# One subtraction of a weight split is queued later on VectorE, at three stage ends of a two-layer decoder trunk

## The chip, the cores and the metric

The kernel runs on one NeuronCore of a Trainium2 chip. The metric is the device time of one execution in microseconds. A core has five engines that work through their own instruction queues: TensorE (PE, with its weight loads listed as PEld), VectorE (DVE), ScalarE (ACT), GpSimd (POOL) and SyncE (SP); the last two mostly issue DMA transfers here. Engines wait for each other by semaphores. An instruction that waits holds up everything behind it on its engine.

## The reference

The program is a decoder trunk of two layers, width 1024, on 512 tokens, in float32. One layer is

```
hn = rms_norm(h, g_ffn1) * (1 + sc1) + sh1
h  = h + 0.5 * (1 + gt1) * (silu(hn @ W_gate) * (hn @ W_up)) @ W_out      # ffn1
hn = rms_norm(h, g_mix) * (1 + sc2) + sh2
h  = h + (1 + gt2) * concat(attention, rwkv7, short_conv)(hn @ W_mix) @ W_mixout
hn = rms_norm(h, g_ffn2) * (1 + sc3) + sh3
h  = h + 0.5 * (1 + gt3) * (silu(hn @ W_gate') * (hn @ W_up')) @ W_out'   # ffn2
```

`sh`, `sc` and `gt` come from a small product with the condition vector `c`. The feed-forward width is 2816.

## The kernel before

**Data.** Activations lie with channels on the 128 partitions and the 512 tokens along the free dimension: the residual `h` is eight channel blocks of 128x512. Float32 products are made of three TensorE products each: every operand is parted into a high half (rounded to the format that TensorE takes) and a low half (what is left), and `mm3` (L125) issues high x high (L129), high activation low half x high weight (L130) and high activation x low weight (L131). In the profile the halves are `hnH`, `hnL` for the normed rows, `actH`, `actL` for the rows inside a feed-forward stage, and `wH`, `wL` for weights. A set of weights is one 128x1024 tile: eight blocks of 128x128, one per channel block. `split` (L138) parts a set with a cast on ScalarE (L141, writes `wH`) and a subtraction on VectorE (L143, writes `wL`).

**Stages.** Six stages run in turn: ffn1, mix, ffn2 of layer 0 and the same of layer 1. Each ends by computing the normed rows of the next. This text is about the end of a feed-forward stage, which three of the four feed-forward stages have in this form (the last one has no successor and returns earlier).

**The end of a feed-forward stage** (L691 to L731). The last two output blocks, 6 and 7, are computed in halves of the tokens (`HALVES`: the first 256, then the second 256), so that the first half can be normed while the second is still being multiplied. For each half, `residual` (L343) adds block 6 to `h`, then block 7. When a half is complete:

- `stats` sums the squares by a product with ones (`ps_ss`, L273), then takes a root on ScalarE (L275) and a reciprocal on VectorE (L276).
- `spread` brings the reciprocal to all partitions (`ps_rstd`, L283, TensorE).
- `apply` makes the eight channel blocks of normed rows. Per block: VectorE scales `h` (`hn_t`, L290), ScalarE adds the shift and rounds (`hnH`, L291), VectorE takes the low half (`hnL`, L292).

The sum of squares over blocks 0 to 6 is gathered in `ss` on VectorE (L250, after a square on ScalarE, L254); block 7 is added in `stats` itself.

The next stage begins with three sets of weights at once. The end of the stage before loads them into `raws` and `next_weights` splits them: the first set early, the second and the third beside the first half's `stats`. A fourth set is split by the code of the next stage (`load_w`, L299).

**What sets the order.** The code is recorded by a layer that then places each engine's instructions by its own estimate of when they are ready, in the order of the code where nothing else speaks. `queue_behind(name)` (L135) asks for a place behind the instruction last noted under that name: `act` and `dve` are notes of the norm's steps on ScalarE and VectorE, `norm_act` and `norm_dve` of the last L291 and L292. So a moved line in the code can move other instructions too, and the order that was built is what counts.

```
def next_weights(n):
    for w in raws[len(nxt) : n]:
        nxt.append(tuple(wp.tile([P, KD, P], F32R, name=x, tag=x, bufs=4) for x in ("wH", "wL")))
        split(*nxt[-1], w, ("act", "dve"))
```

Of the kernel before, what the change touches and what calls it, by code (L numbers as in the profile page):

```python
# [8 lines left out]
F32 = mybir.dt.float32  # L9
F32R = mybir.dt.float32r  # L10
# [7 lines left out]
P = 128  # L18
# [3 lines left out]
KD = D // P  # L22
# [48 lines left out]
def trunk_kernel(ctx, tc, ins, out, layers=L, phases=("ffn1", "mix", "ffn2")):  # L71
    nc = tc.nc
# [4 lines left out]
    wp = ctx.enter_context(tc.tile_pool(name="wp", bufs=3))  # L77
# [6 lines left out]
    act, mm = nc.scalar.activation, nc.tensor.matmul  # L84
# [10 lines left out]
    def psmm(tags=("mm",)):  # L95
        turn[0] += 1
        return psum([P, T], "ps_mm", tags[turn[0] % len(tags)])
# [27 lines left out]
    def mm3(acc, w, k, x, sl, start, stop):  # L125

        wH, wL, xH, xL = w[0][:, k], w[1][:, k], weave(x[0][:, sl]), weave(x[1][:, sl])
        acc = paired(acc)
        mm(acc, wH, xH, start=start, stop=False)  # L129
        mm(acc, wH, xL, start=False, stop=False)  # L130
        latest["large"] = mm(acc, wL, xH, start=False, stop=stop)  # L131
# [3 lines left out]
    def queue_behind(name):  # L135
        return tc.issue_after(latest[name].ins) if name in latest else nullcontext()

    def split(hi, lo, src, behind=None):  # L138
        a, d = behind or (None, None)
        with queue_behind(a):  # L140
            latest["cast"] = nc.scalar.copy(hi, src)  # L141
        with queue_behind(d):
            return nc.vector.tensor_sub(lo, src, hi.bitcast(F32))  # L143

    ALL = slice(0, T)
    HALVES = (slice(0, T // 2), slice(T // 2, T))
# [78 lines left out]
    def ada_steps(pool, crep, n, behind=None):  # L225

        cols = []
        for _ in todo[:n]:
            ada_turn[0] += 1
            cols.append(ada_load(pool.tile([P, D], F32, name="wada", tag=("first", "third", "sum1")[ada_turn[0] % 3], bufs=1)))  # L230
        ada_sums(cols, crep, behind)


    def ada_until(pool, crep, l, i):
        while todo and todo[0] <= (l, i, KD - 1):
            ada_steps(pool, crep, 1)
# [104 lines left out]
    def residual(pt, i, gate, ss, sl=ALL):  # L341
        hs = inorder(h[i][:, sl])
        done = stt(hs, Woven(pt).view, gate[:, i : i + 1], hs, ALU.mult, ALU.add)  # L343
        add_ss(ss, i, sl)
        return done

    def last_residual(pt, i, gate, ss, sl):

        residual(pt, i, gate, None, sl)
        return None if ss is None else square(i, sl)  # L350

    def ffn(l, w_in, w_pair, w_out, hn, im, ss, need, then, first, ready, coming):
# [6 lines left out]
        with tc.tile_pool(name="act", bufs=1) as ap_:  # L359
# [263 lines left out]
            late = ((5, 0), (7, 1), (10, "P1"), (12, "P2"), (13, "T3"), (14, "T4"))  # L623
# [73 lines left out]
            raws, nxt = [], []  # L697
# [4 lines left out]
            def next_weights(n):  # L702
                for w in raws[len(nxt) : n]:
                    nxt.append(tuple(wp.tile([P, KD, P], F32R, name=x, tag=x, bufs=4) for x in ("wH", "wL")))
                    split(*nxt[-1], w, ("act", "dve"))

            ada_until(ap_, crep, *need)
            stats, spread, apply = then()
            sqs = []
            for sl in HALVES:  # L710
                for i in (6, 7):
                    pt = psmm(BANKS[1:3])[:, : T // 2]
                    for j in range(j0, j1):
                        mm3(pt, last[i, j0 + (j - j0) // n * n], (j - j0) % n, xs[j], sl, j == j0, j == j1 - 1)
                        if sl is HALVES[1]:
                            if (i, j) == (6, j0 + 5):
                                stats(HALVES[0], sqs)
                                next_weights(3)
                            elif (i, j) == (7, j0):
                                spread(HALVES[0])  # L720
                                apply(HALVES[0])
                    if i == 6:
                        residual(pt, i, cg, ss, sl)
                        if sl is HALVES[0]:
                            next_weights(1)
                    else:
                        sqs = [last_residual(pt, i, cg, ss, sl)]
# [891 lines left out]
    for n, (l, p) in enumerate(seq):  # L1619
        im = what[p][1]  # L1620

        coming = ()
        if n + 1 < len(seq):
            l1, p1 = seq[n + 1]
            coming = [ins["wmi"][l1, t] if p1 == "mix" else ins[p1.replace("ffn", "w") + "i"][l1, t // 2, t % 2] for t in range(3)]
        nss = new_ss() if n + 1 < len(seq) else None
        nxt = []

        def then():
            if nss is None:  # L1630
                return [lambda *_: None] * 3
            nhn, scale, *steps = normed(n + 1, nss)
            nxt.append(nhn)
            scale()
            return steps

        if p == "mix":
            with tc.tile_pool(name="mix", bufs=1) as mp:
                ready = mix(l, hn, nss, mp, then, ready) or ()
        else:  # L1640
            w, need = ("w1", (l, 6)) if p == "ffn1" else ("w2", (l + 1, 1))
            ready = ffn(l, ins[w + "i"], ins[w + "p"], ins[w + "o"], hn, im, nss, need, then, first, ready, coming)
        first = None
        hn = nxt[0] if nxt else None
# [86 lines left out]
```

## Time and profile before

| what | value |
|---|---|
| median of 3 timed runs | 1795.22 us (1794.1 to 1796.64) |
| the profiled execution's own time | 1792.58 us |
| its span, first to last instruction | 1790.8 us |
| TensorE busy | 1766.0 us, 99% |
| VectorE busy | 1384.6 us, 77% |
| ScalarE busy | 856.5 us, 48% |
| first feed-forward end (ffn1, layer 0, to mix) | about 340 to 370 us |
| second end (ffn2, layer 0, to ffn1 of layer 1) | about 895 to 924 us |
| third end (ffn1, layer 1, to mix) | about 1224 to 1254 us |

Rows of the timeline give start and duration in us, the engine, the source line, the operation with what it writes and reads, and in brackets how long the engine stood idle before it and what ended that. A row with x2 or x3 is a run of equal instructions. The starts of neighbouring TensorE products lie closer than their durations, since products overlap; the step from start to start is what one costs. Rows of the windows view give, for a stretch of time, the busy time of each engine, the granted TensorE clock (PEclk, 1.00 is full speed) and the DMA share.

### The profile page before, as it was taken

The page shows a single profiled execution, that of the slowest core. Times are in us where ns is not written, and L with a number is a line of the kernel's source. Part 1 is how long each engine was busy: PE and PEld are TensorE (multiplying, and loading weights), DVE is VectorE, ACT ScalarE, POOL GpSimd, SP SyncE. Part 2 cuts the span into 40 slices and gives each one's busy share as a digit, 9 for nine tenths or more (in the row PEclk, how much of TensorE's full clock was granted, in tenths as well). Part 3 has the DMA queues.
Part 4 walks back from the last instruction along what each step waited for, and adds up shares of the span by engine and source line. Part 5 has one row for each costly group of instructions (what it writes and reads, how often), then busy time and mean ns, then how long its engine had stood idle before and what let it go on. Part 6 is the DMA issues. An engine that isn't in the chain of part 4 may idle for free.

```text
span 1790.8 us, 34026 instructions
## 1 busy us (share of the span) xinstructions
PE 1766.0 (99%) x13952; PEld 1613.3 (90%) x13952; DVE 1384.6 (77%) x2224; ACT 856.5 (48%) x1324; POOL 148.3 (8%) x233
## 2 busy tenths in 40 slices
PE   9999999999999999999999999999999999999998
PEld 7898999987778999899899989999877798999998
DVE  7877678867768877677888776887686788864897
ACT  7452354364444554255355514543654345533563
POOL 0101001101000001100100020010000000010000
PEclk9999999999999999999999999999999999999999
DMA  9667867523133666877737687773321427684764
GB/s 378 219 185 265 227 191 214 188 76 91 42 120 100 172 192 219 265 199 202 246 96 203 175 294 199 200 228 116 112 67 39 142 80 204 183 243 133 202 172 112
DMA packets 95436, 313.08 MB, mean 175 GB/s; under 512 B 10864, under 2 KB 13168, under 8 KB 94256
## 3 DMA queue, kind: packets, MB, share of 16 engines
q1 hardware_dynamic: 65088, 203.68, 33.8%
q0 software_dynamic: 30192, 107.23, 24.2%
q8 instruction: 109, 1.79, 0.4%
q14 instruction: 47, 0.39, 0.1%
HBM read 306.93 MB, written 3.93 MB: 174 GB/s over the span
## 4 chain that ended last, share of the span: by engine, by line
PE 85%; DVE 9%; ACT 3%; issue 2%; DMA 2%; SPq 0%; DVEq 0%; ACTq 0%
PE ps_mm L129 14%; PE ps_mm L130 14%; PE ps_mm L131 14%; PE ps_d L434 7%; PE ps_d L436 7%; PE ps_d L435 7%; PE ps_f L436 3%; PE ps_f L435 3%; PE ps_f L434 3%; DVE wL L143 2%; PE ps_mm L1546 2%; PE ps_g L436 2%; PE ps_g L435 2%; PE ps_g L434 2%; ACT wH L141 1%
## 5 line engine op out<-in xcount | busy, mean ns | idle before, releaser
L141 ACT CAST wH<-wraw 128x1024 fp32r<-128x1024 f32 (+2 forms) x276 | 254.3, 928 | 441.1 <-PE ps_mm L130 188.7
L143 DVE TENSOR_TENSOR wL<-wraw,wH 128x1024 fp32r<-128x1024 f32 (+2 forms) x276 | 295.4, 1074 | 112.6 <-ACT wH L141 111.8
L129 PE MATMUL ps_mm<-actH,wH 128*128 128x512 f32 (+1 forms) x700 | 253.6, 362 | 1.0 <-DVE h L343 1.0
L130 PE MATMUL ps_mm<-actL,wH 128*128 128x512 f32 (+1 forms) x700 | 252.8, 361 | 0.0
L131 PE MATMUL ps_mm<-actH,wL 128*128 128x512 f32 (+1 forms) x700 | 252.8, 361 | 0.0
L129 PE MATMUL ps_mm<-hnH,wH 128*128 128x512 f32 (+1 forms) x712 | 248.5, 354 | 3.3 <-ACT hnH L291 3.0
L130 PE MATMUL ps_mm<-hnL,wH 128*128 128x512 f32 (+1 forms) x712 | 246.4, 348 | 0.3
L131 PE MATMUL ps_mm<-hnH,wL 128*128 128x512 f32 (+1 forms) x712 | 245.5, 346 | 0.6 <-DVE wL L143 0.6
L434 PE MATMUL ps_d<-comH,wH 128*128 128x256 f32 x864 | 238.5, 276 | 0.0
L435 PE MATMUL ps_d<-comL,wH 128*128 128x256 f32 x864 | 237.6, 275 | 0.0
L436 PE MATMUL ps_d<-comH,wL 128*128 128x256 f32 x864 | 237.6, 275 | 0.0
L143 DVE TENSOR_TENSOR wL<-sum,wH 128x1024 fp32r<-128x1024 f32 x110 | 134.6, 1225 | 80.3 <-ACT wH L141 80.2
L199 DVE SCALAR_TENSOR_TENSOR wada<-wada,crep 128x1024 f32<-128x1024 f32 x128 | 153.3, 1221 | 31.6 <-DMA wada<-in_wadaT 30.9
L141 ACT CAST wH<-sum 128x1024 fp32r<-128x1024 f32 x110 | 115.1, 1047 | 120.2 <-PE ps_f L435 39.3
L434 PEld LDWEIGHTS ps_d<-comH,wH 128*128 128x128 f32 x864 | 165.8, 192 | 1.7 <-ACT s L460 1.6
L436 PEld LDWEIGHTS ps_d<-comH,wL 128*128 128x128 f32 x864 | 165.9, 192 | 0.0
L435 PEld LDWEIGHTS ps_d<-comL,wH 128*128 128x128 f32 x864 | 165.9, 192 | 0.0
L129 PEld LDWEIGHTS ps_mm<-hnH,wH 128*128 128x128 f32 x712 | 134.2, 191 | 23.7 <-issue 7.6
L131 PEld LDWEIGHTS ps_mm<-hnH,wL 128*128 128x128 f32 x712 | 136.0, 191 | 13.9 <-DVE wL L143 1.0
L130 PEld LDWEIGHTS ps_mm<-hnL,wH 128*128 128x128 f32 x712 | 136.1, 191 | 13.4 <-DVE hnL L292 1.3
L129 PEld LDWEIGHTS ps_mm<-actH,wH 128*128 128x128 f32 x700 | 132.7, 190 | 17.2 <-DVE h L343 1.9
L131 PEld LDWEIGHTS ps_mm<-actH,wL 128*128 128x128 f32 x700 | 132.7, 190 | 15.5
(426 smaller groups left out, 4005.0 us busy)
## 6 DMA issues: line engine op xcount, KB each, us to landing
wada<-in_wadaT POOLq DMA_DIRECT2D x126, 512.0 KB, 4.7
wraw<-in_wmi SPq DMA_DIRECT2D x40, 512.0 KB, 3.5
wraw<-in_w2p SPq DMA_DIRECT2D x36, 512.0 KB, 4.1
wraw<-in_w1p SPq DMA_DIRECT2D x32, 512.0 KB, 4.2
wraw<-in_w1o SPq DMA_DIRECT2D x32, 384.0 KB, 4.9
wraw<-in_w2o SPq DMA_DIRECT2D x32, 384.0 KB, 4.2
wraw<-in_w1o SPq DMA_DIRECT2D x32, 320.0 KB, 3.7
sum<-in_w2p SPq DMA_DIRECT2D x18, 512.0 KB, 4.4
```

Source lines behind the costliest of these rows:

```text
L129: mm(acc, wH, xH, start=start, stop=False)
L130: mm(acc, wH, xL, start=False, stop=False)
L131: latest["large"] = mm(acc, wL, xH, start=False, stop=stop)
L141: latest["cast"] = nc.scalar.copy(hi, src)
L143: return nc.vector.tensor_sub(lo, src, hi.bitcast(F32))
L199: stt(w, w, 1.0, crep, ALU.mult, ALU.mult, accum_out=out_)
L434: mm(acc, wH, xH, start=start and i + k == 0, stop=False, skip_group_check=True)
L435: mm(acc, wH, xL, start=False, stop=False, skip_group_check=True)
L436: mm(acc, wL, xH, start=False, stop=k == 3, skip_group_check=True)
L1546: latest["large"] = pin("PE", mm(paired(pts[n]), w, x, start=first, stop=last, skip_group_check=True))
```

## The change

The third set's split is taken apart. Its cast stays where it was on ScalarE. Its subtraction is asked for behind the first channel block's low half (`norm_dve`, L292) of the first half of the tokens; `apply` is called for block 0 first, then the subtraction is recorded, then `apply` for blocks 1 to 7.

```
+            def third_weights(parts):
+                if not parts:
+                    parts.extend(wp.tile([P, KD, P], F32R, name=x, tag=x, bufs=4) for x in ("wH", "wL"))
+                    with queue_behind("act"):
+                        nc.scalar.copy(parts[0], raws[2])
+                else:
+                    with queue_behind("norm_dve"):
+                        nc.vector.tensor_sub(parts[1], raws[2], parts[0].bitcast(F32))
+                    nxt.append(tuple(parts))
+
...
-            sqs = []
+            sqs, late = [], []
...
                             if (i, j) == (6, j0 + 5):
                                 stats(HALVES[0], sqs)
-                                next_weights(3)
+                                next_weights(2)
+                                third_weights(late)
                             elif (i, j) == (7, j0):
                                 spread(HALVES[0])
-                                apply(HALVES[0])
+                                apply(HALVES[0], range(1))
+                                third_weights(late)
+                                apply(HALVES[0], range(1, KD))
```

In the built program this moves instructions on VectorE, TensorE and, at the two ends before a mix stage, SP. In the changed file lines from here on stand 13 higher, and the moved cast and subtraction have lines of their own (L711, L714).

**VectorE at the first end, from the first half's reciprocal on.** `wL_3563` is the second set's low half, `wL_3567` the third's, `wL_3856` the fourth's. `hn_t` and `hnL` with ascending numbers are the channel blocks in turn. Before:

```order
L276 RECIPROCAL rstd_3559<-rstd_3559 128x2
L143 TENSOR_TENSOR wL_3563<-wraw_3440,wH_3562 128x1024
L143 TENSOR_TENSOR wL_3567<-wraw_3442,wH_3566 128x1024
L343 SCALAR_TENSOR_TENSOR h6_91<-ps_mm_3535,cg_1443,h6_91 128x256
L143 TENSOR_TENSOR wL_3856<-wraw_3854,wH_3855 128x1024
L250 TENSOR_TENSOR ss_578<-ss_578,sq_3583 128x256
L290 SCALAR_TENSOR_TENSOR hn_t_3593<-h0_85,gmod_3460,ps_rstd_3590 128x256
L290 SCALAR_TENSOR_TENSOR hn_t_3597<-h0_85,gmod_3460,ps_rstd_3590 128x256
L290 SCALAR_TENSOR_TENSOR hn_t_3601<-h2_87,gmod_3460,ps_rstd_3590 128x256
L292 SCALAR_TENSOR_TENSOR hnL_3445<-hn_t_3593,mod0_3_1450,hnH_3444 128x256
```

Changed:

```order
L276 RECIPROCAL rstd_3559<-rstd_3559 128x2
L143 TENSOR_TENSOR wL_3563<-wraw_3440,wH_3562 128x1024
L343 SCALAR_TENSOR_TENSOR h6_91<-ps_mm_3535,cg_1443,h6_91 128x256
L290 SCALAR_TENSOR_TENSOR hn_t_3592<-h0_85,gmod_3460,ps_rstd_3589 128x256
L250 TENSOR_TENSOR ss_578<-ss_578,sq_3582 128x256
L290 SCALAR_TENSOR_TENSOR hn_t_3597<-h0_85,gmod_3460,ps_rstd_3589 128x256
L292 SCALAR_TENSOR_TENSOR hnL_3445<-hn_t_3592,mod0_3_1450,hnH_3444 128x256
L714 TENSOR_TENSOR wL_3567<-wraw_3442,wH_3566 128x1024
L292 SCALAR_TENSOR_TENSOR hnL_3447<-hn_t_3597,mod0_3_1450,hnH_3446 128x256
L290 SCALAR_TENSOR_TENSOR hn_t_3601<-h2_87,gmod_3460,ps_rstd_3589 128x256
L290 SCALAR_TENSOR_TENSOR hn_t_3605<-h2_87,gmod_3460,ps_rstd_3589 128x256
```

The third low half went from second to behind block 0's low half, and the fourth, which the change does not name, left this place too. The second and third ends have the same rows in the same order.

**VectorE at the end of the first half's rows, first end.** Before:

```order
L343 SCALAR_TENSOR_TENSOR h6_91<-ps_mm_3586,cg_1443,h6_91 128x256
L292 SCALAR_TENSOR_TENSOR hnL_3459<-hn_t_3621,mod0_3_1450,hnH_3458 128x256
L844 TENSOR_SCALAR omka_3864<-par_93 128x2
L845 TENSOR_SCALAR om_3860<-par_93 128x8
L846 TENSOR_SCALAR w0h_3861<-par_93 128x2
L847 TENSOR_SCALAR a0h_3862<-par_93 128x2
L848 TENSOR_TENSOR gqk_3863<-par_93 128x1
L276 RECIPROCAL rstd_3660<-rstd_3660 128x2
```

Changed:

```order
L343 SCALAR_TENSOR_TENSOR h6_91<-ps_mm_3585,cg_1443,h6_91 128x256
L292 SCALAR_TENSOR_TENSOR hnL_3459<-hn_t_3621,mod0_3_1450,hnH_3458 128x256
L143 TENSOR_TENSOR wL_3856<-wraw_3854,wH_3855 128x1024
L276 RECIPROCAL rstd_3660<-rstd_3660 128x2
L857 TENSOR_SCALAR omka_3864<-par_93 128x2
```

The fourth low half now stands here, ahead of the second half's reciprocal.

**TensorE at the first end, where the next stage's products begin.** `ps_mm_3707`, `3708` and `3709` are the sums of the first, second and third set. Before:

```order
L273 MATMUL ps_ss_3655<-ones_r_100,ss_578 128x1
L129 MATMUL ps_mm_3707<-hnH_3444,wH_3497 128x256
L129 MATMUL ps_mm_3708<-hnH_3444,wH_3562 128x256
L129 MATMUL ps_mm_3709<-hnH_3444,wH_3566 128x256
L130 MATMUL ps_mm_3707<-hnL_3445,wH_3497 128x256
L131 MATMUL ps_mm_3707<-hnH_3444,wL_3498 128x256
L130 MATMUL ps_mm_3708<-hnL_3445,wH_3562 128x256
L131 MATMUL ps_mm_3708<-hnH_3444,wL_3563 128x256
L130 MATMUL ps_mm_3709<-hnL_3445,wH_3566 128x256
L131 MATMUL ps_mm_3709<-hnH_3444,wL_3567 128x256
```

Changed:

```order
L273 MATMUL ps_ss_3655<-ones_r_100,ss_578 128x1
L129 MATMUL ps_mm_3707<-hnH_3444,wH_3497 128x256
L130 MATMUL ps_mm_3707<-hnL_3445,wH_3497 128x256
L131 MATMUL ps_mm_3707<-hnH_3444,wL_3498 128x256
L129 MATMUL ps_mm_3708<-hnH_3444,wH_3562 128x256
L130 MATMUL ps_mm_3708<-hnL_3445,wH_3562 128x256
L131 MATMUL ps_mm_3708<-hnH_3444,wL_3563 128x256
L129 MATMUL ps_mm_3709<-hnH_3444,wH_3566 128x256
L130 MATMUL ps_mm_3709<-hnL_3445,wH_3566 128x256
L131 MATMUL ps_mm_3709<-hnH_3444,wL_3567 128x256
```

The third set's low half is used last of the nine in both. Of the nine products, the first now needs only block 0's high half and the second already its low half. Further on, at the first two ends, `ps_rstd` of the second half stands nine products (one channel block) later than before, and so one block nearer to the first product of that half. At the third end the third set's sum has no free bank yet, and the first half's products run over the first two sets alone until later, in both programs.

**SP.** At the two ends before a mix stage, the load of the fifth set (`wraw_3974` at the first end), which takes over the buffer that the fourth set's split frees, moves behind the small load `lw`. At the second end SP keeps its order. GpSimd's queue is the same everywhere.

## The prediction

> **What bounds the kernel now.** First the page, then the waits of TensorE over the whole run, longest total first.
>
> ```profile
> span 1790.8 us, 34026 instructions
> PE 1766.0 (99%) x13952; PEld 1613.3 (90%) x13952; DVE 1384.6 (77%) x2224; ACT 856.5 (48%) x1324; POOL 148.3 (8%) x233
> ...
> PE ps_mm L129 <- ACT hnH L291: 3.0, 5, 0.7
> PE ps_ss L273 <- DVE ss L250: 2.4, 4, 0.7
> ```
>
> TensorE is busy 99% of the span, so only its remaining waits can be won. The two largest are waits for the norm's rows: for `hnH` and for `ss`. Three of their four or five places are the ends that the change touches. So I read the timeline there. TensorE at the first end:
>
> ```profile
> 349.53 0.28 PE L131 MATMUL ps_mm<-actH,wL 128*128 128x256 f32 x1
> 350.40 0.38 PE L273 MATMUL ps_ss<-ones_r,ss 128*128 128x1 f32 x2 [0.59 <-DVE ss L250]
> 351.33 0.60 PE L129 MATMUL ps_mm<-hnH,wH 128*128 128x256 f32 x3 [0.55 <-ACT hnH L291]
> 351.97 0.38 PE L130 MATMUL ps_mm<-hnL,wH 128*128 128x256 f32 x1
> 352.18 0.28 PE L131 MATMUL ps_mm<-hnH,wL 128*128 128x256 f32 x1
> ...
> 354.29 0.42 PE L129 MATMUL ps_mm<-hnH,wH 128*128 128x256 f32 x1
> 354.50 0.42 PE L130 MATMUL ps_mm<-hnL,wH 128*128 128x256 f32 x1
> ...
> 357.05 0.28 PE L129 MATMUL ps_mm<-hnH,wH 128*128 128x256 f32 x1
> 357.16 0.28 PE L130 MATMUL ps_mm<-hnL,wH 128*128 128x256 f32 x1
> ```
>
> A 128x256 product costs 0.11 us from start to start at full rate (357.05, 357.16). From the stage's last product at 349.53 to the first `hnL` product at 351.97 pass 2.44 us, in which one product, two short ones for `ps_ss` (at most 0.11 each) and three `hnH` products stand: 0.66 us of work. So 1.78 us are lost, and about 0.1 more because the first product after a wait takes 0.21 to the next start (351.97 to 352.18): **1.9 us**. VectorE and ScalarE in the same place show what was late:
>
> ```profile
> 346.12 2.36 DVE L143 TENSOR_TENSOR wL<-wraw,wH 128x1024 fp32r<-128x1024 f32 x2 [0.77 <-ACT wH L141]
> 348.40 0.48 DVE L343 SCALAR_TENSOR_TENSOR h<-ps_mm,cg,h 128x256 f32<-128x256 f32 x1
> 348.79 1.22 DVE L143 TENSOR_TENSOR wL<-wraw,wH 128x1024 fp32r<-128x1024 f32 x1
> 349.92 0.42 DVE L250 TENSOR_TENSOR ss<-ss,sq 128x256 f32<-128x256 f32 x1
> 350.26 1.26 DVE L290 SCALAR_TENSOR_TENSOR hn_t<-h,gmod,ps_rstd 128x256 f32<-128x256 f32 x3
> 351.43 0.48 DVE L292 SCALAR_TENSOR_TENSOR hnL<-hn_t,mod,hnH 128x256 fp32r<-128x256 f32 x1
> ...
> 345.05 2.93 ACT L141 CAST wH<-wraw 128x1024 fp32r<-128x1024 f32 x3
> 348.97 0.42 ACT L254 ACTIVATE sq<-h 128x256 f32<-128x256 f32 x1 [0.99 <-DVE h L343]
> 350.77 1.31 ACT L291 ACTIVATE hnH<-hn_t,mod 128x256 fp32r<-128x256 f32 x3 [1.39 <-DVE hn_t L290]
> ```
>
> VectorE has no idle time from 346.12 on: three low halves of weights stand ahead of `ss` and of the first `hn_t`, and TensorE waits for both. The other two ends have the same shape, first and last row each:
>
> ```profile
> 904.31 0.28 PE L131 MATMUL ps_mm<-actH,wL 128*128 128x256 f32 x1
> 906.75 0.38 PE L130 MATMUL ps_mm<-hnL,wH 128*128 128x256 f32 x1
> ...
> 1234.44 0.28 PE L131 MATMUL ps_mm<-actH,wL 128*128 128x256 f32 x1
> 1236.88 0.38 PE L130 MATMUL ps_mm<-hnL,wH 128*128 128x256 f32 x1
> ```
>
> Again 2.44 us each: 1.9 us lost at the second end, and 2.0 at the third, where only two `hnH` products stand in it.
>
> There is a second loss. At 354.29 the same product steps by 0.21 us. The windows view around the three waits:
>
> ```profile
> 349.02:352.43 3.41, 2.23 (x17) 1.76 (x16) 3.41 (x8) 1.76 (x5) 0.99 (x2) 1.00 0.37 109
> 352.43:355.85 3.42, 3.42 (x19) 3.42 (x18) 3.42 (x10) 1.95 (x4) 0.00 (x0) 0.50 0.24 85
> ...
> 901.98:905.39 3.41, 2.82 (x26) 2.63 (x24) 3.41 (x6) 1.20 (x2) 0.00 (x0) 1.00 0.00 0
> 905.39:908.81 3.42, 2.83 (x23) 2.56 (x23) 3.42 (x10) 2.45 (x6) 0.00 (x0) 1.00 0.46 153
> 1233.07:1236.49 3.42, 2.28 (x19) 2.00 (x18) 3.42 (x8) 1.23 (x3) 0.98 (x2) 1.00 0.14 17
> ```
>
> Behind the first end's wait the granted clock is 0.50 for 3.42 us; behind the other two it stays at 1.00, after waits of the same length. Taking the columns after the length, TensorE was busy 2.23 us of the 3.41 before the slow stretch, and 2.28 or more in the others. So a wait like this one is near what halves the clock, and where it falls in time decides. The price is 3.42 x (1 - 0.11/0.21) = **1.6 us**.
>
> [...]
>
> **The change, part by part.** Nothing is added or removed: the same cast, the same subtraction, the same products. The built order moves two low halves (the third and the fourth) behind the first rows. Steps on VectorE from the rows above, start to start: a weight's low half 1.14 us (348.40 - 346.12, halved), a 128x256 row 0.39 (three in 1.26, the last 0.48 long), `ss` 0.34.
>
> First end, new order. Second set's low half 346.12, `h` 347.26, block 0's `hn_t` 347.65. `ss` now waits for ScalarE: its third cast ends at 347.98, the square takes 0.42 behind it, so `ss` starts at about 348.4 and ends at 348.8 instead of 350.3. `hn_t` of block 1 348.7, `hnL` of block 0 349.1 to 349.6, third low half 349.5 to 350.7, `hnL` of block 1 350.6 to 351.1, then `hn_t` of blocks 2 to 4 from 351.0, `hnL` of block 2 352.2 to 352.7. ScalarE has block 0's `hnH` by 348.8. The casts hide nothing new: ScalarE's order is unchanged.
>
> TensorE is free at 349.64, and everything for the first eight next-stage products is ready. `ps_ss` 0.22 and eight products 0.89 bring it to 350.75, where the third low half is due (350.7 plus the 0.06 that a row takes to reach TensorE, 349.92 + 0.42 to 350.40): 0.1 us of wait and 0.1 for the restart. Block 1's `hnL` at 351.15 costs another 0.2, block 2's at 352.7 another 0.35. After that VectorE makes a block every 0.8 us and TensorE uses one in nine products, 1.0 us: it no longer catches up. So 0.75 us instead of 1.9.
>
> What the move makes late: the second half's first rows. `ps_rstd` stands one block nearer to them:
>
> ```profile
> 360.18 0.43 PE L283 MATMUL ps_rstd<-con,rstd 128*128 128x128 f32 x2
> 360.65 1.26 DVE L290 SCALAR_TENSOR_TENSOR hn_t<-h,gmod,ps_rstd 128x256 f32<-128x256 f32 x3 [0.53 <-PE ps_rstd L283]
> 361.16 1.31 ACT L291 ACTIVATE hnH<-hn_t,mod 128x256 fp32r<-128x256 f32 x3 [1.24 <-DVE hn_t L290]
> ```
>
> From 360.18 to the first `hnH` at about 361.7 pass 1.5 us. Today 18 products (2.0 us) cover that; then nine and the rstd itself, 1.2 us: a new wait of about 0.3 plus 0.1 for the restart. In return `ps_rstd`, which waits about 0.2 us today, has products enough ahead of it. Net cost 0.2. The end gains 1.9 - 0.75 - 0.2, about 1.0; the second, with the same order, also 1.0. At the third end only two sets' products stand between the blocks, so TensorE meets VectorE sooner: waits of 0.6 (block 1's `hnL`), 0.5 and 0.4 (block 2's `hnH` and `hnL`), 1.5 in all against 2.0 and some three restarts of 0.1 today (its products already wait on `hnL` block by block), and the second `ps_rstd`, as at the first end, 0.2: a gain of 1.0. Together **3.0 us**. The bounds: nothing, if the waits only change their name, and 5.8, if all of 1.9, 1.9 and 2.0 went; I take the middle because every step of it has a row.
>
> The fourth low half, now ahead of the second reciprocal, ends near 357.3, when the root is also due; with nine products in between it costs nothing. Moved back with it is the fifth set's load, whose buffer it frees:
>
> ```profile
> 350.04 0.33 SPq L304 DMA_DIRECT2D wraw<-in_wmi  x1
> ...
> wraw<-in_wmi SPq DMA_DIRECT2D x40, 512.0 KB, 3.5
> ...
> 372.58 1.05 ACT L141 CAST wH<-wraw 128x1024 fp32r<-128x1024 f32 x1
> ```
>
> It would be issued near 357.4 and land by 361; its cast is the one at 372.58. Eleven microseconds of slack: nothing.
>
> Clock: at the first two ends the new waits are short and parted by products, 0.75 us of them within any 3.41, so TensorE is busy some 2.7 us there, well above the 2.28 that kept full clock. At the third end 1.5 us of waits fall within 2.5 us: that stays near 2.3, where it is today. So one slow stretch goes in the profiled execution: **1.6 us**. For the timed runs I know only that their median lies 2.6 us above the profiled 1792.58, which leaves room for one more such stretch. Bounds 0 and 4.8 (three); I take one.
>
> Sum: 3.0 + 1.6 = 4.6. Against the profiled execution, 1792.58 with its span of 1790.8, that is 1788.0; against the median, 1795.22 - 4.6 = **1790.6**.
>
> **The rivals.** (a) *Only the waits shrink*: the timed runs' clock is not helped, because their slow stretches lie elsewhere or come back. For it: two of three ends run at full clock in the profile, and the third end's new waits stay near the edge. 1795.22 - 3.0 = 1792.2. [...]
>
> (b) *The wait is handed on*: block 1's `hnL` behind the third low half, and the second half's rows, cost as much as was won. For it: VectorE has no idle time before 356, so the same work must pass. Against: TensorE needs only block 0 to begin, and the two moved rows are not needed for 1 us and 18 us. 1795.22 - 0.7, about 1794.5.
>
> (c) *Slower*: the fourth low half delays the second reciprocal. Place: VectorE, between block 7's `hnL` and L276. It decides if the root is ready before that row starts; then `ps_rstd` waits up to 1.14 us, the second half's rows too, and with the 0.4 of the second half's first row it comes near the 1.9 that halved the clock. Price: 3 x 1.14 = 3.4 of wait and 3 x 1.6 = 4.8 of slow clock, with only the 3.0 of the first half won: 1795.22 + 5.2 = 1800.4. Against: by the times above root and row end within 0.2 us of each other, and nine products stand between.
>
> **How the numbers follow.** Forecast 0.62, (a) 0.22, (b) 0.09, (c) 0.07. What this kernel's measurement can tell from no change is about 0.2%, 3.6 us: faster means below 1791.6, slower above 1798.8. The forecast spreads by one slow stretch downward (1789.0) and by a third of its first term upward (1791.6): faster in nearly all of it; with a third of (a), which lies close to the line, that is 0.68 faster. (b) and the rest of (a) are the 0.25 of no change, and (c) is the 0.07. The range runs from three stretches saved in the timed runs, 1787.4, to halfway between (a) and (b), 1793.4; it leaves out (c) and most of (b).
>
> **What would show it.** In the changed profile: at each end `ss` (L250) starts 1.5 us sooner and TensorE's wait for it is gone; the first `hnL` product follows the stage's last product by well under 1 us; a wait of 0.1 to 0.3 us for L714 or block 1's `hnL`; a new wait of some 0.3 us at the second half's first `hnH`; no granted clock of 0.50 at the three ends. The forecast is wrong if the sum of TensorE's idle time at an end stays near 1.9 us, or if the clock still halves with it reduced.

## The result and the profile after

| | before | after |
|---|---|---|
| median of the runs compared | 1795.56 us (1792.99 to 1797.2, 8 runs) | 1790.17 us (1788.12 to 1791.26, 8 runs) |
| ratio, with 95% interval | | 0.9976 (0.9967 to 0.9984) |
| the profiled execution, its own time | 1792.58 us | 1788.12 us |
| its span | 1790.8 us | 1786.4 us |

The change makes the kernel 0.24% faster by the ratio on record; the two medians by themselves give 0.9970, which lies in its interval. The forecast was 1790.6 us, and 1788.0 for a profiled execution like the one shown before. One run below, of second_early, took 1819.12 us at a mean clock of 0.949, where every other run has 0.996 or more; it is left out of all medians, ratios and counts.

The head of the page after the change, and its waits of TensorE over the whole run (line, what it waited for, us in total, times, longest):

```profile
span 1786.4 us, 34022 instructions
PE 1764.7 (99%) x13952; PEld 1611.1 (90%) x13952; DVE 1385.0 (78%) x2224; ACT 856.1 (48%) x1324; POOL 148.6 (8%) x233
...
PE ps_mm L129 <- ACT hnH L291: 1.5, 3, 0.7
```

The wait for `hnH` is half of what it was, and the three that are left are two at the ends of the mix stages and one of 0.2 us at the third end. The wait for `ss`, 2.4 us before, is 0.4 us, once, at the end of the first mix stage.

VectorE at the first end, after:

```profile
345.09 0.17 DVE L276 RECIPROCAL rstd<-rstd 128x2 f32<-128x2 f32 x1 [2.67 <-ACT rstd L275]
346.02 1.22 DVE L143 TENSOR_TENSOR wL<-wraw,wH 128x1024 fp32r<-128x1024 f32 x1 [0.77 <-ACT wH L141]
...
348.24 0.42 DVE L250 TENSOR_TENSOR ss<-ss,sq 128x256 f32<-128x256 f32 x1 [0.20 <-ACT sq L254]
...
348.98 0.48 DVE L292 SCALAR_TENSOR_TENSOR hnL<-hn_t,mod,hnH 128x256 fp32r<-128x256 f32 x1
349.37 1.22 DVE L714 TENSOR_TENSOR wL<-wraw,wH 128x1024 fp32r<-128x1024 f32 x1
...
356.02 1.22 DVE L143 TENSOR_TENSOR wL<-wraw,wH 128x1024 fp32r<-128x1024 f32 x1
357.50 0.17 DVE L276 RECIPROCAL rstd<-rstd 128x2 f32<-128x2 f32 x1 [0.26 <-ACT rstd L275]
```

One low half (346.02) stands ahead of `ss` instead of three. The third is the row at 349.37, the fourth the one at 356.02.

TensorE in the same place:

```profile
349.44 0.28 PE L131 MATMUL ps_mm<-actH,wL 128*128 128x256 f32 x1
...
349.69 0.36 PE L129 MATMUL ps_mm<-hnH,wH 128*128 128x256 f32 x1
349.88 0.28 PE L130 MATMUL ps_mm<-hnL,wH 128*128 128x256 f32 x1
...
350.55 0.28 PE L130 MATMUL ps_mm<-hnL,wH 128*128 128x256 f32 x1
350.66 0.36 PE L131 MATMUL ps_mm<-hnH,wL 128*128 128x256 f32 x1
350.86 0.28 PE L129 MATMUL ps_mm<-hnH,wH 128*128 128x256 f32 x1
351.04 0.38 PE L130 MATMUL ps_mm<-hnL,wH 128*128 128x256 f32 x1
...
352.04 0.54 PE L129 MATMUL ps_mm<-hnH,wH 128*128 128x256 f32 x3
352.61 0.38 PE L130 MATMUL ps_mm<-hnL,wH 128*128 128x256 f32 x1
...
359.27 0.28 PE L131 MATMUL ps_mm<-hnH,wL 128*128 128x256 f32 x1
359.66 0.82 PE L129 MATMUL ps_mm<-hnH,wH 128*128 128x256 f32 x4
```

The first `hnL` product now follows the stage's last product by 0.44 us, where it took 2.44. No row has a bracket; the small waits have to be read from the steps. 350.66 to 350.86 is 0.20 where a product costs 0.11: the third low half was just due. 350.86 to 351.04 is 0.18, so 0.07 us went to block 1's low half. 352.04 to 352.61 is 0.57 for three products that cost 0.33 together, so 0.24 us went to block 2's. 359.27 to 359.66 is 0.39, so 0.28 us went to the second half's first row.

**What an end costs, read to 0.02 us.** The runs differ by a microsecond or two elsewhere, so the ends are compared by a length inside one execution: from the start of the first half's reciprocal (L276) to the start of the first 128x512 product L131 of the next stage. Between the two stand, in every kernel here, the same 37 products of the old stage and 146 of the next (before_fill, below, adds nine). At the second end, before and after:

```profile
899.97 0.17 DVE L276 RECIPROCAL rstd<-rstd 128x2 f32<-128x2 f32 x1 [1.79 <-ACT rstd L275]
...
924.19 0.38 PE L131 MATMUL ps_mm<-hnH,wL 128*128 128x512 f32 x1
```

```profile
897.27 0.17 DVE L276 RECIPROCAL rstd<-rstd 128x2 f32<-128x2 f32 x1 [2.67 <-ACT rstd L275]
...
920.50 0.38 PE L131 MATMUL ps_mm<-hnH,wL 128*128 128x512 f32 x1
```

924.19 - 899.97 = 24.22 us before, 920.50 - 897.27 = 23.23 after. The same for all ends and all kernels of this text, each value the difference of two such starts:

| kernel | first end | second end | third end |
|---|---|---|---|
| before | 25.75 | 24.22 | 24.66 |
| before, second profile (before_look_1) | 24.22 | 25.74 | 24.65 |
| before, third profile (before_look_2) | 24.22 | 24.22 | 24.66 |
| after | 23.23 | 23.23 | 23.66 |
| after, second profile (changed_again) | 23.21 | 23.22 | 23.66 |
| fourth_only | 23.18 | 23.18 | 23.51 |
| third_only | 24.12 | 24.11 | 24.66 |
| before_fill, before_fill_again | 24.23, 24.22 | 24.22, 24.23 | 24.66, 24.66 |
| second_early, second_early_again | 22.49, 22.48 | 22.49, 22.48 | 22.48, 22.49 |
| second_early_third_late | 22.50 | 22.47 | 22.60 |

The change takes 0.99, 0.99 and 1.00 us off the three ends, against the 24.22 and 24.66 without a slow stretch: 3.0 us. The two values near 25.75 hold a slow stretch of the clock, which costs 1.53 us (25.75 - 24.22). For the profiled executions 3.0 + 1.53 = 4.5, and their spans differ by 4.4.

### The profile page after: what moved, and what is told of

Its sections match the earlier page's. It is cut to its first block, busy times and chain, and to the rows that moved or that the text cites. A ratio compares the mean times of both kernels' runs of the same rounds, so it can differ in the third digit from the quotient of the medians.

```text
span 1786.4 us, 34022 instructions
## 1 busy us (share of the span) xinstructions
PE 1764.7 (99%) x13952; PEld 1611.1 (90%) x13952; DVE 1385.0 (78%) x2224; ACT 856.1 (48%) x1324; POOL 148.6 (8%) x233
## 4 chain that ended last, share of the span: by engine, by line
PE 86%; DVE 8%; ACT 3%; issue 1%; DMA 1%; SPq 0%; DVEq 0%; ACTq 0%
PE ps_mm L129 14%; PE ps_mm L130 14%; PE ps_mm L131 14%; PE ps_d L434 7%; PE ps_d L435 7%; PE ps_d L436 7%; PE ps_f L436 3%; PE ps_f L435 3%; PE ps_f L434 3%; PE ps_mm L1559 2%; PE ps_g L435 2%; PE ps_g L434 2%; PE ps_g L436 2%; DVE wL L143 2%; ACT wH L141 1%
## 5 line engine op out<-in xcount | busy, mean ns | idle before, releaser
L143 DVE TENSOR_TENSOR wL<-wraw,wH 128x1024 fp32r<-128x1024 f32 (+2 forms) x273 | 291.4, 1071 | 106.6 <-ACT wH L141 105.3
L131 PE MATMUL ps_mm<-actH,wL 128*128 128x512 f32 (+1 forms) x700 | 252.8, 361 | 0.0
L131 PE MATMUL ps_mm<-hnH,wL 128*128 128x512 f32 (+1 forms) x712 | 244.8, 346 | 0.6 <-DVE wL L143 0.6
L131 PEld LDWEIGHTS ps_mm<-hnH,wL 128*128 128x128 f32 x712 | 135.2, 190 | 14.2 <-DVE wL L143 1.0
L131 PEld LDWEIGHTS ps_mm<-actH,wL 128*128 128x128 f32 x700 | 132.7, 190 | 15.6
```

## The experiments

### Which of the two moved rows pays

The change moves the third low half by its own lines, and the scheduling layer then also takes the fourth back. Two kernels part them. *fourth_only* starts from the kernel before; the first piece is in `apply`, the second in `projector`:

```
+                if sl is HALVES[0]:
+                    latest["first_half"] = latest["dve"]
...
+        if ready and len(ws) == 3:
+            ws.append(load_w(srcs[3], behind=(None, "first_half")))
         fetch(n0 + ahead)
```

> The third low half is back in its old place, second on VectorE behind the first reciprocal; the fourth set's split alone goes late, to the same place as in the changed kernel (ahead of the second half's reciprocal). Theory A, the fourth's leaving is what pays: until block 2's low half VectorE has the same rows to do whether the third stands first or in between, so TensorE's idle time is as after the change, in another order: at the first two ends some 0.3 us for ss (L250), 0.15 for block 0's low half and 0.3 for the second half's first high half, about 1.0 us each with the restarts, 1.5 at the third; the time is that of the changed kernel, 1789 to 1791.5. Theory B, the third's own move pays: with it undone ss comes 1.14 us sooner than before instead of 1.5, two rows stand ahead of it, and half of the gain or less is left: 1792.5 to 1794.

Measured: 1789.29 us (11 runs), ratio 0.9981 (0.9972 to 0.9990); ends 23.18, 23.18, 23.51. VectorE and TensorE at the first end:

```profile
345.80 2.36 DVE L143 TENSOR_TENSOR wL<-wraw,wH 128x1024 fp32r<-128x1024 f32 x2 [0.77 <-ACT wH L141]
...
349.10 0.43 DVE L250 TENSOR_TENSOR ss<-ss,sq 128x256 f32<-128x256 f32 x1 [0.15 <-ACT sq L254]
...
350.62 0.48 DVE L292 SCALAR_TENSOR_TENSOR hnL<-hn_t,mod,hnH 128x256 fp32r<-128x256 f32 x1
```

```profile
349.58 0.38 PE L273 MATMUL ps_ss<-ones_r,ss 128*128 128x1 f32 x2
349.82 0.58 PE L129 MATMUL ps_mm<-hnH,wH 128*128 128x256 f32 x3
350.37 0.38 PE L130 MATMUL ps_mm<-hnL,wH 128*128 128x256 f32 x1
```

With two low halves still ahead, `ss` starts 4.24 us behind the reciprocal (349.10, the reciprocal at 344.86), 1.1 us later than after the change (348.24 - 345.09 = 3.15). TensorE waits 0.26 us for it (349.21 to 349.58, where a product takes 0.11) and 0.2 for block 0's low half (349.82 to 350.37, less three products), with a restart of 0.1 behind it. But behind them VectorE has nothing left but the rows (350.62 is block 1's low half), and no further wait comes in the first half. The second half's first row is waited for as after the change (359.00 to 359.38, 0.28 us too long).

*third_only* starts from the changed kernel; the fourth set is loaded and split by the end of the stage, so that its low half stands ahead of `ss` again (the lines that hand its weights on are left out here):

```
                 if not parts:
                     ...
                         nc.scalar.copy(parts[0], raws[2])
+                    fourth.append(load_w(coming[3], behind=("act", "dve")))
...
-            return nxt
+            return nxt + fourth
```

> The third low half stands behind block 0's low half as in the changed kernel; the fourth is asked for where it stood before, among the rows ahead of ss. Theory A: VectorE has one low half more to do ahead of block 1's rows, 1.14 us; TensorE starts the next stage early but then waits 0.3 us for the third low half, 0.7 for block 1's high half and 0.2 for its low half: 2.2 us at the first two ends and 2.7 at the third, as before the change; 1794 to 1796.5, or 1.6 lower for each slow stretch of the clock that the other spread of the waits saves. Theory B: ss is early, most of the gain stays: 1790.5 to 1792.5.

Measured: 1792.59 us (11 runs), ratio 0.9996 (0.9987 to 1.0005), no difference that can be told; ends 24.12, 24.11, 24.66. VectorE and TensorE at the first end:

```profile
348.00 1.22 DVE L143 TENSOR_TENSOR wL<-wraw,wH 128x1024 fp32r<-128x1024 f32 x1
349.13 0.42 DVE L250 TENSOR_TENSOR ss<-ss,sq 128x256 f32<-128x256 f32 x1
...
349.86 1.22 DVE L715 TENSOR_TENSOR wL<-wraw,wH 128x1024 fp32r<-128x1024 f32 x1
351.00 1.26 DVE L290 SCALAR_TENSOR_TENSOR hn_t<-h,gmod,ps_rstd 128x256 f32<-128x256 f32 x3
```

```profile
349.85 0.47 PE L129 MATMUL ps_mm<-hnH,wH 128*128 128x256 f32 x2
...
351.13 0.38 PE L131 MATMUL ps_mm<-hnH,wL 128*128 128x256 f32 x1
352.07 0.60 PE L129 MATMUL ps_mm<-hnH,wH 128*128 128x256 f32 x3 [0.55 <-ACT hnH L291]
```

The next stage starts early (349.85). TensorE then waits 0.3 us for the third low half (350.71 to 351.13), and when block 0's nine products are done 0.8 us for block 1 (351.13 to 352.07): its `hn_t` stands behind the fourth, `ss`, block 0's low half and the third, at 351.00.

By the lengths theory A holds to 0.15 us at each end, and B falls. The times alone would not decide it for third_only: its 1792.59 us lie between A's range and B's, and the kernel before stood at 1793.22 in that comparison. The fourth's leaving is worth 1.04, 1.04 and 1.15 us by itself; the third's new place 0.10, 0.11 and 0.00 by itself, and it costs 0.05, 0.05 and 0.15 once the fourth is gone. What counts is how many rows VectorE has between the first reciprocal and block 2's low half, not which of them stands first. The line that the change names hardly pays; what it set off in the scheduling layer does.

### Another row out of the stretch

If VectorE's work in that stretch is the bound, a third low half taken out of it must pay again. Before the reciprocal VectorE is idle for 2.67 us (the bracket at 345.09 above). *second_early* is fourth_only with one line more:

```
                             if (i, j) == (6, j0 + 5):
+                                next_weights(2)
                                 stats(HALVES[0], sqs)
                                 next_weights(3)
```

> The third low half in its old place, the fourth late as in fourth_only, and the second set's split asked for ahead of the first half's root instead of behind it, into the 2.7 us in which VectorE is idle before the first reciprocal (ScalarE 1.9 us before the root). Theory A (the bound is VectorE's work between that reciprocal and block 2's low half): another 1.14 us leaves the stretch, ss and block 0's rows are ready when TensorE ends the stage, and its waits fall from 1.0 us an end to 0.1 to 0.4, from 1.5 to about 0.5 at the third: some 2.4 us under the changed kernel. Against: the second low half delays the first reciprocal by 0.1 us, and ps_rstd with it; if that chain bounds the first rows, no gain.

> The version with the second set's split ahead of the root and the fourth late, with more runs. In its first profile each end took 2.03 us less than before, against 0.85 for the change. Ratio to the kernel before 0.9955 to 0.9968, 1786 to 1788.

Measured: ratio 0.9963 (0.9950 to 0.9975) and 0.9964 (0.9950 to 0.9977), medians 1786.62 (5 runs) and 1786.37 us (7 runs); ends 22.48 or 22.49 at all three, 1.74, 1.74 and 2.18 us under the kernel before and 2.7 us in all under the changed one, where 2.4 was expected. (The 0.85 and 2.03 us an end that two of the expectations name do not come out of this length, which gives 0.99 to 1.00 and 1.74 to 2.18.) VectorE, then TensorE at the first end:

```profile
344.01 1.22 DVE L143 TENSOR_TENSOR wL<-wraw,wH 128x1024 fp32r<-128x1024 f32 x1 [1.48 <-ACT wH L141]
345.20 0.17 DVE L276 RECIPROCAL rstd<-rstd 128x2 f32<-128x2 f32 x1
346.13 1.23 DVE L143 TENSOR_TENSOR wL<-wraw,wH 128x1024 fp32r<-128x1024 f32 x1 [0.77 <-ACT wH L141]
...
348.30 0.43 DVE L250 TENSOR_TENSOR ss<-ss,sq 128x256 f32<-128x256 f32 x1 [0.15 <-ACT sq L254]
```

```profile
349.54 0.28 PE L131 MATMUL ps_mm<-actH,wL 128*128 128x256 f32 x1
...
349.80 0.36 PE L129 MATMUL ps_mm<-hnH,wH 128*128 128x256 f32 x1
349.99 0.28 PE L130 MATMUL ps_mm<-hnL,wH 128*128 128x256 f32 x1
...
355.20 0.38 PE L273 MATMUL ps_ss<-ones_r,sq 128*128 128x1 f32 x2
```

The second low half ends just as the root arrives, and nothing is lost there: the reciprocal starts 0.30 us behind the start of the root (344.90 to 345.20), as in the changed kernel (344.79 to 345.09). At the first two ends every row of the first half is ready before TensorE asks for it. One wait is left there, 0.3 us for the second half's square (354.79 to 355.20, where a product takes 0.11); at the third end two restarts of 0.1 at `hnL` rows are left. So all three ends now cost the same, but something is still to be won at each. This version beats both kernels.

*second_early_third_late* makes the same move in the changed kernel (`next_weights(2)` ahead of `stats`, then `third_weights`).

> The changed kernel with the second set's split ahead of the first half's root. Theory A: with one low half less in the stretch the third's place no longer matters; the third is done before TensorE asks for it in either place, so this equals second_early within 0.5 us. If the third's own place behind block 0 counts (theory B), it is faster than second_early by 0.3 us an end or more.

Measured: ratio 0.9964 (0.9951 to 0.9977), ends 22.50, 22.47 and 22.60. With one row less in the stretch the third's place does not matter, save at the third end, where it costs 0.1 us, and where the reciprocal is another 0.12 us late behind its root, which this length leaves out (0.42 us from 1224.35 to 1224.77, for 0.30).

### The clock

The prediction took one slow stretch of 1.6 us away, because the one in the profile stood behind the first end's wait. In the trace of that profile (before) the record of the granted clock changes at 352.434, 355.847 and 1789.445 us: the slow stretch is 3.413 us long, and the last two changes lie 1433.598 us apart, 420.04 times that length (420 steps of 3.4133). So there the changes fall on a grid of 3.41 us, as far as one such distance can show it; a window here is one step of it, and the phase is where the steps lie in an execution. Two more profiles of the kernel before ask whether the slow stretch is a matter of the place or of the phase.

> The kernel before once more, for a second profile. The waits at the three ends are set by the order of the rows and stay as they were (0.59 us for ss, 0.55 for the first high half). Whether the clock halves behind them goes by where the 3.41 us windows of this execution fall: if that is so, the stretch of 0.50 stands at another place, or at several, or nowhere, while the waits are the same; if it goes by the place alone, it stands behind the first end again and at no other.

> The same as before_look_1, for a third profile of the kernel before.

Measured: in one the stretch stands behind the second end, in the other at none; the waits of 3.0 us for `hnH` are the same in both. The windows around the second end of the first of them (length, busy time of PE, PEld, DVE, ACT and POOL, then the granted clock):

```profile
905.56:908.98 3.42, 2.24 (x16) 1.78 (x15) 3.42 (x9) 1.77 (x5) 0.00 (x0) 1.00 0.43 145
908.98:912.39 3.41, 3.41 (x18) 3.41 (x18) 3.41 (x10) 1.90 (x5) 0.00 (x0) 0.50 0.02 8
```

It is the picture of the first end in the prediction, with 2.24 us busy for 2.23 and idle times of 0.59 and 0.55 us in both, one end later. At the second end in the prediction the boundary between two windows, 905.39, cut the waits in two (2.82 and 2.83 us busy); here one window holds both. So with the same waits the halving moved to another end, with the windows, and of nine passages through these ends in three profiles two were hit (the values of 25.75 and 25.74 in the table). After the change none of six was, in two profiles, and TensorE is busy in more of each window (the first end's and the third's, 421 and 162 steps ahead of the change at 1784.82 in the trace of after):

```profile
347.81:351.22 3.41, 3.41 (x31) 3.30 (x30) 3.21 (x7) 1.31 (x4) 0.43 (x1) 1.00 0.00 0
1231.86:1235.27 3.41, 2.84 (x20) 2.22 (x19) 3.41 (x10) 1.82 (x4) 0.98 (x2) 1.00 0.12 38
```

For the timed runs there is only the mean clock of each: one stretch of 3.41 us at half speed in 1790 lowers it by 0.001 (3.41 x 0.5 / 1790). *changed_again* runs the changed kernel beside others.

> The changed kernel itself, beside the kernel before and the others on one chip. From the first profile: 0.85 us less at each end than before. For the clock: a window of 3.41 us at the ends now holds at least 1.7 us of streaming products wherever its phase lies, so these ends should halve the clock in no run; the runs' mean clocks should show fewer stretches than those of the kernel before (about one a run), not none, since the mix ends keep their waits. Ratio to the kernel before 0.9970 to 0.9985.

Measured: 1789.99 us (9 runs), ratio 0.9978 (0.9968 to 0.9987). Its profile has one slow stretch, behind the end of the first mix stage, at 570.59. The mean clocks of the timed runs that have one on record:

| kernel | runs | 1.000 | 0.999 | 0.998 | 0.997 or less | stretches a run |
|---|---|---|---|---|---|---|
| before | 66 | 14 | 33 | 13 | 6 | 1.2 |
| after | 17 | 6 | 11 | 0 | 0 | 0.65 |
| fourth_only | 11 | 8 | 3 | 0 | 0 | 0.3 |
| third_only | 11 | 5 | 5 | 1 | 0 | 0.6 |
| second_early and second_early_again | 12 | 9 | 3 | 0 | 0 | 0.25 |

The last column counts each 0.001 as a stretch; with clocks given to 0.001 and so few runs it is rough (fourth_only and the changed kernel should be alike). It also pools three comparisons, in which the kernel before has 1.0, 1.4 and 1.25 stretches a run. Pooled, the change takes away about 0.55 of a stretch a run. In the one comparison with both kernels' clocks, that of changed_again, it is 30 stretches in 21 runs against 5 in 9, so 0.9. With 1.53 us each that is 0.8 to 1.3 us, where the prediction took 1.6; so few runs do not tell it from one stretch.

Runs of equal mean clock, all comparisons together, part the clock's share from that of the ends:

| mean clock | before | after | apart |
|---|---|---|---|
| 1.000 | 1791.75 us (14 runs) | 1788.95 (6) | 2.8 |
| 0.999 | 1793.20 (33) | 1790.24 (11) | 3.0 |

So the 3.0 us of the ends stand in the timed runs too, and what a saving has beyond them goes with the clock. The kernel before also gives the price of a stretch once more, 1.45 us from row to row. Together the two shares are 3.8 to 4.3 us, 0.21 to 0.24% of 1795, inside the intervals of both comparisons (0.9967 to 0.9984 and 0.9968 to 0.9987).

*before_fill* tries the clock's share by itself: nine products more in the waits of the kernel before, written into a sum that the first real product overwrites.

```
             pts = [psum([P, T], "ps_mm", tag) for tag in first]
+            if ready:
+                w = ws[0][0]
+                for _ in range(9):
+                    with tc.issue_after(latest["large"].ins):
+                        mm(pts[0][:, : T // 2], w[:, 0], w[:, :2].rearrange("p k n -> p (k n)"), start=True, stop=True)
```

> The kernel before, with nine products more at each of the three ends, three ahead of ps_ss and six behind it, in the time in which TensorE waited for ss and for the first high half; they write into the bank of the next stage's first sum, which the first real product overwrites. All other rows stand as before, so the waits for the rows of the norm stay and only their idle time is filled. If the clock term of the prediction is right for the timed runs, no granted clock of 0.50 is left at the three ends and the time falls by 1.6 us for each slow stretch, and by at most 0.1 an end for the restart: 1793 to 1794.5. If the timed runs owe nothing to the clock there, 1795 to 1796.

> The filled kernel before, for a second profile and more runs. In its first profile the three ends ran at full clock and all of the gain was lost in the second mix stage, where ss came 1.1 us late and the clock halved at 1456 us. If that was chance, the profile now has the 1.5 us of the first end and nothing lost behind it, 1789 to 1791.5 in the profiled execution; if the fill itself brings it on, the same rows show again.

Measured: ratio 1.0004 (0.9995 to 1.0013) and 1.0007 (0.9998 to 1.0015). At the three ends it did what was meant: the table shows 24.22 and 24.66 with no stretch in either profile. But the time did not fall, and the mean clocks did not rise: the 21 timed runs hold 23 stretches, 1.1 a run. In both profiles the end of the second mix stage, where nothing was added, lost more than the first end had won: from its first 128x256 product to the second half's reciprocal it took 19.38 us (1448.68 to 1468.06) and 19.91 (1449.85 to 1469.76), for 16.74 before (1449.69 to 1466.43). In the first of them:

```profile
1446.23 1.06 ACT L141 CAST wH<-wraw 128x1024 fp32r<-128x1024 f32 x1 [0.83 <-DMA wraw<-in_w2i]
...
1454.90 0.38 PE L273 MATMUL ps_ss<-ones_r,ss 128*128 128x1 f32 x2 [1.14 <-DVE ss L250]
```

A cast waited 0.83 us (0.94 in the second profile, there put down to a product), TensorE then 1.14 for `ss` (1.20). Behind it, from the first half's reciprocal to the second's, pass 11.27 us (1456.79 to 1468.06; 11.36 in the second profile), for 9.69 or 9.70 in the three profiles of the kernel before; that is 1.58 and 1.67 longer, about what a slow stretch costs (1.53), and the mean clocks of the two profiled runs, 0.999 and 0.998, leave room for one and for two. None of the three profiles of the kernel before shows that wait at this place; one has as long a wait for `ss` at the end of the first mix stage. Whether the added products bring it on is open, so the clock's share of the timed runs rests on the counts and the equal clocks above and not on this kernel.

*after_fill_mix* puts six such products into the waits at the ends of the two mix stages of the changed kernel (`if not ready`, `range(6)`).

> The changed kernel with six products more at the ends of the two mix stages (565 to 575 us and near 1455), behind the stage's last product, where TensorE still waits 0.66 us for the first high half; they too are overwritten. Six of the eight runs of the changed kernel have a mean clock of 0.999, which is one slow stretch of 3.4 us in 1787, and these take about 1.6 us longer than the two at 1.000. If that stretch belongs to the mix ends, it goes and the time is 1788 to 1789; if it lies elsewhere, 1790 as the changed kernel.

Measured: 1789.0 us (11 runs), ratio 0.9981 (0.9972 to 0.9990), not to be told from the changed kernel's 0.9976 and 0.9978. Its profile has no slow stretch and 7 of its 11 runs a mean clock of 1.000. (The 1.6 us that the expectation gives for a mean clock of 0.999 come out as 2.1 by the means of those six and two runs, 1790.46 and 1788.37.) But fourth_only, without these products, has 8 of 11 in the same comparison, so this does not show the mix ends to be the place of the remaining stretch.

## Why the prediction was right, and where it was not

**The ends: right, at 1.0 us each.** The waits at the first end, with their restarts, were put at 0.2 for the third low half, 0.2 for block 1's, 0.35 for block 2's and 0.3 for the second half's first row before its restart; the steps give 0.09, 0.17 (0.07 + 0.10), 0.35 (0.24 + 0.11) and 0.28. `ss` starts 1.6 us sooner (349.92 to 348.24, less the 0.09 by which this execution was ahead), where 1.5 was said. The sum of 3.0 us was measured as 2.98. Its part for the third end is not as sure as it looks: 1.0 comes out there only if the 0.2 of the second `ps_rstd` counts as a gain (2.0 + 0.3 - 1.5 + 0.2); as the net cost that it is at the first end, the same terms give 0.6. The trace after shows no wait for the second half's first row at that end, which fits the 1.00 that was measured.

**What that sum did not say** is which row earns it. The prediction followed the built order as a whole and so priced both moves together. By its words "TensorE needs only block 0 to begin" one would credit the early start. third_only has that early start and gains 0.2 us in all, so crediting it would have been wrong, and that the total came out is owed to pricing the two moves as one. The right reading was the sentence beside it, that VectorE has no idle time before 356: rows must leave that stretch, and it is the fourth that left.

**The clock: right for the profiled execution, a guess and somewhat large for the timed runs.** 1.53 us was measured for the stretch taken as 1.6, and it went. That the profiled execution held one at these ends was chance: of three profiles of the kernel before, one holds none there. For the median, "I take one" was a guess, and on the large side: by the counts 0.55 to 0.9 of a stretch a run goes, 0.8 to 1.3 us for 1.6, since the ends hold less than one a run and some stretch stays elsewhere. Rival (a), waits alone, gives 1792.2 and the forecast 1790.6; a saving of 3.8 to 4.3 us lies between them. The measured medians, 1795.56 and 1790.17 in one comparison and 1793.6 and 1789.99 in the other, lie 5.4 and 3.6 apart, which is how far such medians scatter.

**The third end.** "1.5 us of waits fall within 2.5 us: that stays near 2.3" failed: the window there has 2.84 us busy. TensorE in it:

```profile
1231.76 0.39 PE L129 MATMUL ps_mm<-hnH,wH 128*128 128x256 f32 x2
1232.35 0.38 PE L130 MATMUL ps_mm<-hnL,wH 128*128 128x256 f32 x1 [0.20 <-DVE hnL L292]
...
1232.79 0.28 PE L131 MATMUL ps_mm<-hnH,wL 128*128 128x256 f32 x1
1233.28 0.49 PE L129 MATMUL ps_mm<-hnH,wH 128*128 128x256 f32 x2 [0.22 <-ACT hnH L291]
1233.92 0.38 PE L130 MATMUL ps_mm<-hnL,wH 128*128 128x256 f32 x1
```

By the steps the waits are what was worked: 0.37 (1231.76 to 1232.35, less two products), 0.38 (1232.79 to 1233.28, less one) and 0.42 (1233.28 to 1233.92, less two), with the restarts behind the two `hnL` 1.4 us for the 1.5 that was said. But a product lasts 0.28 to 0.38 us where it costs 0.11 from start to start, and its tail counts as busy: of 0.37 and 0.38 the brackets show 0.20 and 0.22. A sum of steps cannot be taken off a window's busy time.

**The rivals.** (b) fell: at the first end 0.6 us of waits stayed instead of 1.9, and with the second half's first row 0.3 to 0.4 came new. It was right about the place, though; with the fourth left where it was it would have come true (third_only). (c) did not come about: the fourth low half ends at 357.24 (356.02 + 1.22), the reciprocal waits 0.26 us more for its root, at all three ends, and so the margin was a quarter of a microsecond. The fifth set's load is issued at 357.33 as worked, and its cast comes at 370.19.

## What to carry to other kernels

When a schedule moves more than the edit names, undo each move by itself before crediting the edit: here the named one earned next to nothing. Where an engine is saturated in front of a hand-over, count the rows between its last idle time and the first thing that is waited for, and take rows out of that stretch, backward into idle time if there is any; their order within it is worth a tenth as much. A length between two rows of one execution, with the same work between them, told 0.05 us apart where whole runs scatter by 2 us.

## What the runs showed of the hardware that was not expected

The busy time of TensorE in a window did not tell whether the clock would halve behind it. The prediction's limit between 2.23 and 2.28 us is refuted from both sides. In changed_again it halved behind 2.92 us, at the end of the first mix stage (a place with twelve `ps_ss` products of one column, 569.50 to 570.86 in before_look_2):

```profile
567.17:570.59 3.42, 2.92 (x26) 2.73 (x25) 3.06 (x5) 1.31 (x2) 0.00 (x0) 1.00 0.43 128
570.59:574.00 3.41, 3.29 (x17) 3.21 (x16) 0.98 (x4) 0.42 (x2) 0.00 (x0) 0.50 0.56 179
```

In third_only it did not halve behind 2.11 us, with an idle time of 1.30 us in one piece:

```profile
1232.34:1235.75 3.41, 2.11 (x17) 1.82 (x15) 3.41 (x8) 0.92 (x3) 0.99 (x2) 1.00 0.51 159
1235.75:1239.17 3.42, 3.27 (x28) 3.05 (x27) 3.42 (x10) 1.93 (x5) 0.00 (x0) 1.00 0.11 33
```

Two products of one column count as busy for 0.38 us (349.58 in fourth_only), and a product of 256 columns lasts 0.28 us where it steps by 0.11, so the busy time is no count of the work in a window. A count of the 256-column products that start in it, from the timeline rows, gives 12 in each of two windows behind which the clock halved (349.02 before, 905.56 in before_look_1), 13 in third_only's at 1232.34 and 15 in that of before at 1233.07, behind which it did not. The 1.7 us that the expectation of changed_again takes as enough are an estimate of this kind: 15 products at 0.11 us are 1.65. Four windows that lie one to three products apart do not show a limit, and no run was made to test one: what halves the clock stays open.
